# Sliding windows of an image batch: the second batch half shifted by one stride in SBUF, and half of each tile stored by SyncE

## The chip, the cores and the metric

The kernel runs on one core of a Trainium2 chip. The metric is the device time of one execution in microseconds. Before the change it is 185.93 us, the median of 3 runs (185.61 to 186.04). Engines are called as in the profile: DVE (VectorE), ACT (ScalarE), POOL (GpSimd), SP (SyncE, which only issues transfers here). The core has 16 DMA engines that all queues share.

## The reference

The input is 16 images of 64 channels and 64 x 64 pixels in float32. The output holds all windows of 8 x 8 pixels at a stride of 4, 15 x 15 of them, each with all channels:

```python
for i in range(n_h):          # n_h = n_w = 15
    for j in range(n_w):
        h_start = i * stride
        w_start = j * stride
        result[:, i, j] = x[:, :, h_start:h_start + 8, w_start:w_start + 8].copy()
```

Nothing is computed. 16.8 MB are read and 16 x 225 x 64 x 64 x 4 bytes = 59.0 MB are written. One output row, that is one window of one image with all channels, is 16 KB and contiguous in memory.

## The kernel before, in words

**Layout.** The input is loaded once into a tile `Lt`. A partition (lane) holds one image's band of 16 pixel rows for half of the channels: lane = channel half x 64 + image x 4 + band, with 4 bands per image. Images 0 to 7 (y = 0) and 8 to 15 (y = 1) therefore lie in groups of 32 lanes: channel half 0 has y = 0 in lanes 0 to 31 and y = 1 in 32 to 63, channel half 1 has them in 64 to 95 and 96 to 127. Each channel takes 1024 + 32 floats of a lane (L50 to L52).

**Loads.** The first 8 channels of each half are staged: ACT's and SP's queues load them into the four tile buffers `GG` (L115 to L118), and DVE and ACT copy them from there into `Lt` (L131 to L135). All other channels go straight to `Lt` (L120 to L126), in transfers of 8 lanes, by POOL's queue and six of them by SP's.

**Tiles.** The output is made in tiles of 128 lanes x 16 KB, each lane being one output row. There are four buffers in rotation (`tile_`, L193). DVE and ACT copy the windows of a tile out of `Lt` (both channel halves into one lane), and then one store sends the tile out. The vertical window positions of a band are slots s = 0 to 3 of the horizontal position j; s = 3 reaches four pixel rows into the next band, so its lower half comes from the next lane, by a `stream_shuffle` that moves lanes by one (`nxt`, L138). Tiles with such rows are called crossing here, the others inside the bands.

**Stores.** A tile leaves by an indirect transfer on POOL's queue (`scatter`, L146): each lane's target row is an index in a small tile (`idx` and others, computed on DVE in L75 to L104) plus a constant for s and j. An index out of range is dropped by the bounds check. That is used for the last band's crossing rows, which do not exist.

**Order.** The tiles are written out by hand. First three tiles of y = 0 alone (`part`, L198, two slots and two positions j at once), while the second half still loads. Then three times one full tile (`unit`, s = 0 in one half of the lanes and s = 1 in the other) and one `part` of y = 1. Then the loop (L237): three crossing tiles (s = 2 in one half of the lanes, s = 3 in the other, turning from tile to tile) and one inside the bands, five times. In the loop DVE copies by `stream_shuffle` with a mask that keeps each lane where it is (`shf`, L176). Last come two tiles of 64 lanes for j = 14, which SP stores with a plain transfer (L246 to L256):

```python
def unit(j, s, copies=(shf, mix)):
    g = tile_()
    if s == 0:
        fill(g, 0, 0, j, 0, HP, (act, copies[0]))
        fill(g, 1, 1, j, 0, HP, (act, copies[1]))
        scatter(g, idx, j, s)
    else:
        turn = 1 - crossed % 2
        fill(g, turn, s, j, 0, HP, (act, act))
        fill(g, 1 - turn, s + 1, j, 0, HP, (shf, mix))
        scatter(g, (idx_hi, idx_lo)[turn], j, s)
```

A fill of a buffer waits until the store four tiles earlier has landed. A store waits for all of its tile's copies. Stores do not wait for each other.

Of the kernel before, what the change touches and what calls it, by code (L numbers as in the profile page):

```python
# [10 lines left out]
def kernel(  # L11
# [7 lines left out]
    nc = tc.nc  # L19
# [30 lines left out]
    PAD = W // 2  # L50
    Lt = lpool.tile([P, CL, RB * W + PAD], f32)
# [16 lines left out]
    pi, tb, tq, tc_, th, idx, idx_y0, idx_y1, idx_lo, idx_hi = (  # L68
        itile(n) for n in ("pi", "tb", "tq", "tc", "th", "idx", "idx_y0", "idx_y1", "idx_lo", "idx_hi")
    )  # L70
    FAR = float(2 * B * NWIN)
    nc.gpsimd.iota(pi[:, :], pattern=[[0, 1]], base=0, channel_multiplier=1)  # L72
# [4 lines left out]
    def mul(d, a, m):  # L77
        nc.vector.tensor_scalar(out=d[:, :], in0=a[:, :], scalar1=float(m), scalar2=None, op0=ALU.mult)  # L78

    def tt(d, a, b, op):  # L80
        nc.vector.tensor_tensor(out=d[:, :], in0=a[:, :], in1=b[:, :], op=op)  # L81

    bits(tb, 2, B - 1)
    bits(tq, 0, HQ - 1)
    bits(tc_, 6, 1)
    mul(tb, tb, NWIN)
    mul(th, tq, NSLOT * NW)
    tt(tb, tb, th, ALU.add)
    mul(th, tc_, NW)
    tt(idx, tb, th, ALU.add)  # L90

    bits(th, 5, 1)
    mul(idx_y0, th, 1 - YB * NWIN)
    tt(idx_y0, idx_y0, idx, ALU.add)
    nc.vector.tensor_scalar(out=idx_y1[:, :], in0=idx_y0[:, :], scalar1=float(YB * NWIN), scalar2=None, op0=ALU.add)

    nc.vector.tensor_scalar(out=tq[:, :], in0=tq[:, :], scalar1=float(HQ - 1), scalar2=FAR, op0=ALU.is_equal, op1=ALU.mult)
    tt(th, tc_, tq, ALU.mult)
    tt(idx_hi, idx, th, ALU.add)
    nc.vector.tensor_scalar(out=tc_[:, :], in0=tc_[:, :], scalar1=-1.0, scalar2=1.0, op0=ALU.mult, op1=ALU.add)  # L100
    tt(th, tc_, tq, ALU.mult)
    tt(idx_lo, tb, th, ALU.add)
    mul(th, tc_, NW)
    tt(idx_lo, idx_lo, th, ALU.add)  # L104
# [7 lines left out]
    FC = NG * TC // CH  # L112
# [7 lines left out]
    for y in range(NY):  # L120
        for q in range(HQ):
            hw = y * HQ + q < HWP
            if hw:
                load(nc.sync, 0, y, q, FC + SMALL, CL)
# [54 lines left out]
    def split(k, other):  # L179
# [3 lines left out]

        return both

    mix = split(CL // 4, shf)


    EARLY = 3
# [102 lines left out]
```

## Time and profile before

| | |
|---|---|
| median of 3 runs | 185.93 us |
| the profiled execution | 186.0 us |
| its span in the profile | 184.2 us |
| DVE, ACT, POOL busy | 154.0 us (84%), 150.6 us (82%), 50.3 us (27%) |
| bytes moved by DMA | 75.81 MB |
| last DVE copy ends | about 175 us |

The profile shows one execution. Busy time of an engine is time in its instructions. The DMA row gives the busy share of the 16 DMA engines in each of 40 slices of the span, and queues are listed with the time that their packets took: `software_dynamic` is POOL's queue, the `hardware_dynamic` ones are SP's (q1) and ACT's (q10). A group of instructions is one line of the code, one engine and one shape, with the count, the busy sum, the mean of one in ns, and the idle time ahead of it with what ended that. A DMA issue's time to landing reaches from the issuing instruction until the last byte has been acknowledged. Beside the page, the trace holds a record of every DMA packet: its start, length, size and queue.

### The profile page before, as it was taken

How to read it: one execution, taken by the hardware profiler on the slowest of the kernel's cores; microseconds unless marked ns; L12 is line 12 of the kernel's file. 1: busy time of each engine (PE TensorE's matmuls, PEld its weight loads, DVE VectorE, ACT ScalarE, POOL GpSimd, SP SyncE). 2: the span in 40 equal slices, each digit the busy share in tenths (PEclk: the TensorE clock that was granted, in tenths of full speed). 3: DMA queues.
4: the chain of work that ended last, by engine and by line, in shares of the span. 5: the costliest groups of instructions: out<-in, count | busy, mean ns of one | idle time of the engine just before them, and what ended most of it. 6: DMA issues, size and time to landing. Idle time of an engine off the chain costs nothing.

```text
span 184.2 us, 597 instructions
## 1 busy us (share of the span) xinstructions
DVE 154.0 (84%) x213; ACT 150.6 (82%) x100; POOL 50.3 (27%) x50
## 2 busy tenths in 40 slices
DVE  5002998999989897999999999999999999999800
ACT  0002999999999999999899999998999999999600
POOL 7400763033353526111121112111211121114000
DMA  5999999999999999999999999999999999999995
GB/s 141 396 413 408 412 412 412 395 396 441 425 430 430 430 434 427 434 432 430 434 422 438 423 434 438 423 441 413 443 416 427 434 423 413 427 420 406 420 430 235
DMA packets 10980, 75.81 MB, mean 411 GB/s; under 512 B 3280, under 2 KB 3280, under 8 KB 7376
## 3 DMA queue, kind: packets, MB, share of 16 engines
q0 software_dynamic: 8656, 65.55, 84.8%
q1 hardware_dynamic: 1744, 8.13, 10.9%
q10 hardware_dynamic: 576, 2.10, 3.2%
q14 instruction: 4, 0.03, 0.0%
HBM read 16.78 MB, written 62.91 MB: 433 GB/s over the span
## 4 chain that ended last, share of the span: by engine, by line
DVE 53%; DMA 28%; issue 10%; POOL 2%; DVEq 1%; PEldq 0%
DVE GG L177 24%; DVE GG L170 16%; DMA out_dram<-GG,idx_y 14%; DMA Lt<-in_x_dram 14%; DVE GG L206 10%; DVE GG L254 3%; POOL Lt L61 2%; DVE GG L182 0%; DVEq L287 0%; DVE GG L167 0%; POOL pi L72 0%; DVEq L206 0%; PEldq L287 0%
## 5 line engine op out<-in xcount | busy, mean ns | idle before, releaser
L167 ACT COPY GG<-Lt 64x2048 f32<-64x2048 f32 x46 | 87.2, 1897 | 4.2 <-DMA out_dram<-GG,idx 1.8
L177 DVE STREAM_SHUFFLE GG<-Lt 64x1024 f32<-64x1024 f32 (+4 forms) x39 | 52.8, 1355 | 1.3
L206 DVE COPY GG<-Lt 32x2048 f32<-32x2048 f32 x30 | 36.6, 1219 | 3.4 <-DMA out_dram<-GG,idx_y 2.2
L170 DVE STREAM_SHUFFLE GG<-Lt 64x1024 f32<-64x1024 f32 x30 | 38.5, 1285 | 0.0
L206 ACT COPY GG<-Lt 32x2048 f32<-32x2048 f32 x18 | 34.1, 1897 | 0.8 <-DMA out_dram<-GG,idx_y 0.4
L135 DVE COPY Lt<-GG 32x2048 f32<-32x2048 f32 x10 | 11.9, 1234 | 13.8 <-DMA GG<-in_x_dram 13.7
L61 POOL DMA_DIRECT2D Lt<-in_x_dram x16 | 13.7, 868 | 17.8 <-DMA Lt<-in_x_dram 17.3
L147 POOL DMA_INDIRECT out_dram<-GG,idx_y x6 | 10.1, 1690 | 26.3 <-DVE GG L206 17.6
L147 POOL DMA_INDIRECT out_dram<-GG,idx x8 | 11.7, 1463 | 17.5 <-DVE GG L177 13.3
L147 POOL DMA_INDIRECT out_dram<-GG,idx_lo x8 | 7.7, 964 | 30.2 <-DVE GG L170 15.1
L135 ACT ACT_TABLE_LOAD x1 | 1.3, 1283 | 17.3 <-DMA GG<-in_x_dram 17.3
L147 POOL DMA_INDIRECT out_dram<-GG,idx_hi x7 | 6.7, 963 | 26.5 <-ACT GG L167 11.4
L135 ACT COPY Lt<-GG 32x2048 f32<-32x2048 f32 x6 | 11.2, 1894 | 0.1
L181 ACT COPY GG<-Lt 64x256 f32<-64x256 f32 (+2 forms) x21 | 10.2, 484 | 0.5
L167 DVE COPY GG<-Lt 64x2048 f32<-64x2048 f32 x6 | 7.3, 1222 | 0.2
L254 ACT COPY GG<-Lt 32x768 f32<-32x768 f32 x8 | 6.6, 828 | 0.1
L254 DVE COPY GG<-Lt 32x1280 f32<-32x1280 f32 x8 | 6.6, 819 | 0.1
L75 DVE TENSOR_SCALAR tb<-pi 128x1 int32<-128x1 int32 x1 | 0.2, 154 | 1.0 <-POOL pi L72 1.0
L182 DVE COPY GG<-Lt 64x1280 f32<-64x1280 f32 x1 | 0.9, 875 | 0.0
L81 DVE TENSOR_TENSOR th<-tc,tq 128x1 int32<-128x1 int32 x2 | 0.3, 156 | 0.0
L78 DVE TENSOR_SCALAR th<-tc 128x1 int32<-128x1 int32 x2 | 0.3, 154 | 0.0
L72 POOL IOTA pi<- 128x1 int32 x1 | 0.1, 125 | 0.4 <-PEq L287 0.4
(21 smaller groups left out, 3.1 us busy)
## 6 DMA issues: line engine op xcount, KB each, us to landing
Lt<-in_x_dram POOLq DMA_DIRECT2D x10, 768.0 KB, 17.9
Lt<-in_x_dram SPq DMA_DIRECT2D x6, 640.0 KB
GG<-in_x_dram SPq DMA_DIRECT2D x4, 512.0 KB, 14.8
GG<-in_x_dram ACTq DMA_DIRECT2D x4, 512.0 KB, 14.5
out_dram<-GG SPq DMA_DIRECT2D x2, 1024.0 KB, 9.5
Lt<-in_x_dram POOLq DMA_DIRECT2D x6, 128.0 KB, 17.8
out_dram<-GG,idx POOLq DMA_INDIRECT x8, 11.9
out_dram<-GG,idx_lo POOLq DMA_INDIRECT x8, 9.5
```

The costliest lines, as they stand in the source:

```text
L61: eng.dma_start(out=L[p0 : p0 + QP - HQ + 1 : HQ, c0:c1, :, :], in_=x_v[ch, y, q, :, c0:c1, :])
L78: nc.vector.tensor_scalar(out=d[:, :], in0=a[:, :], scalar1=float(m), scalar2=None, op0=ALU.mult)
L81: nc.vector.tensor_tensor(out=d[:, :], in0=a[:, :], in1=b[:, :], op=op)
L135: tc.keep_in_program_order(copy(out=L[d, c : c + PC, :, :], in_=S[ch][f, c : c + PC]))
L147: st = nc.gpsimd.indirect_dma_start(out=o_v, out_offset=bass.IndirectOffsetOnAxis(ap=ix[:, 0:1], axis=0), in_=g.rearrange("p c r w -> p (c ...
L167: copy(out=g[d, cs, :, :], in_=L[f, :, s * ST : s * ST + WS, cols])
L170: nc.vector.stream_shuffle(out=g[d, cs, ST:WS, :], in_=L[f, :, 0:ST, cols], mask=nxt)
L177: nc.vector.stream_shuffle(out=out, in_=in_, mask=same)
L181: act(out=out[:, 0:k], in_=in_[:, 0:k])
L182: other(out=out[:, k:], in_=in_[:, k:])
L206: (act if n % 3 == 0 else dve)(out=g[d * QP : (d + 1) * QP, ch * CL : (ch + 1) * CL, :, :], in_=L[f : f + QP, :, s * ST : s * ST + WS, cols],)
L254: copy(out=g[d, ch * CL + c0 : ch * CL + c1, :, :], in_=L[f, c0:c1, s * ST : s * ST + WS, cols])
```

## The change

The second batch half (y = 1) is stored four elements, which is one stride, further on in each channel of `Lt`, and the two batch halves change places in the lanes. `L` becomes two views of the same tile, `L[0]` from element 0 and `L[1]` from element 4. A copy that runs over 64 lanes of `L[0]` at position j reads window j of y = 0 and window j - 1 of y = 1; over `L[1]` it reads window j of y = 1 and window j + 1 of y = 0.

So a full tile is one slot s for all lanes: the first 64 lanes come from `L[0]`, the others from `L[1]`, and the middle 64 lanes (32 to 95) hold window j of all 16 images, in the order of one plain transfer. In tiles inside the bands (s = 0, 1, 2) SP stores the middle 64 lanes, and a scatter with the index `sw` stores the outer 64, whose middle indices are out of range. Crossing tiles (s = 3) go out by one scatter with the index `sx`. Positions j go in steps of two; the tiles at the edges (j = 0 or 6, and j = 14) fill 96 lanes and have indices of their own.

The copies of a tile inside the bands are one of 2048 elements by ACT, two by DVE's plain copy, and one shared half and half. In a crossing tile ACT copies the upper four rows of all four parts, and DVE shuffles the lower four. The copies by a shuffle that keeps the lanes, and the two half tiles at the end, are gone. One channel fewer of the upper channel half is staged (7 instead of 8), and POOL's loads of that half grow by one channel. The index arithmetic on DVE has 29 instructions instead of 20. The early tiles (`part`) stay.

```diff
-    L = Lt[:, :, 0 : RB * W].rearrange("p c (r w) -> p c r w", r=RB)
+    L = [Lt[:, :, n * ST : n * ST + RB * W].rearrange("p c (r w) -> p c r w", r=RB) for n in range(2)]
...
+    def lanes(ch, y):
+        p0 = ch * HP + (NY - 1 - y) * QP
+        return slice(p0, p0 + QP)
...
     def load(eng, ch, y, q, c0, c1):
-        p0 = ch * HP + y * QP + q
-        eng.dma_start(out=L[p0 : p0 + QP - HQ + 1 : HQ, c0:c1, :, :], in_=x_v[ch, y, q, :, c0:c1, :])
+        p0 = lanes(ch, y).start + q
+        eng.dma_start(out=L[y][p0 : p0 + QP - HQ + 1 : HQ, c0:c1, :, :], in_=x_v[ch, y, q, :, c0:c1, :])
...
-    FC = NG * TC // CH
+    FC = (NG * TC // CH, NG * TC // CH - 1)
...
-            load(nc.gpsimd, 1, y, q, FC, CL)
+            load(nc.gpsimd, 1, y, q, FC[1], CL)
...
-    ACT_C = 12
+    ACT_C = CL // 2
...
-    def unit(j, s, copies=(shf, mix)):
-        nonlocal crossed
+    o_e = out.rearrange("b i j c r w -> j b i (c r w)")
+
+    def unit(j, s):
         g = tile_()
-        if s == 0:
-            fill(g, 0, 0, j, 0, HP, (act, copies[0]))
-            fill(g, 1, 1, j, 0, HP, (act, copies[1]))
-            scatter(g, idx, j, s)
-        else:
-            turn = 1 - crossed % 2
-            crossed += 1
-            fill(g, turn, s, j, 0, HP, (act, act))
-            fill(g, 1 - turn, s + 1, j, 0, HP, (shf, mix))
-            scatter(g, (idx_hi, idx_lo)[turn], j, s)
+        lo = j > (2 * EARLY if s < 2 else 0)
+        hi = j < NW - 1
+        cross = s == NSLOT - 1
+        cols = slice(j * ST, j * ST + WS)
+        for h in range(CH):
+            a, b = (0 if lo else QP, HP) if h == 0 else (0, HP if hi else QP)
+            d = slice(h * HP + a, h * HP + b)
+            for n, ch in enumerate((h, 1 - h)):
+                f = slice(ch * HP + a, ch * HP + b)
+                cs = slice(ch * CL, (ch + 1) * CL)
+                if cross:
+                    act(out=g[d, cs, 0:ST, :], in_=L[h][f, :, s * ST : RB, cols])
+                    nc.vector.stream_shuffle(out=g[d, cs, ST:WS, :], in_=L[h][f, :, 0:ST, cols], mask=nxt)
+                else:
+                    copy = (act, dve, dve, split(ACT_C))[h * CH + n]
+                    copy(out=g[d, cs, :, :], in_=L[h][f, :, s * ST : s * ST + WS, cols])
+        g_q = g.rearrange("p c r w -> p (c r w)")
+        if not cross:
+            free(nc.sync.dma_start(out=o_e[j, :, s : s + (HQ - 1) * NSLOT + 1 : NSLOT], in_=g_q[QP : QP + HP]))
+        outer = ((sw, sx), (sw_lo, sx_lo), (sw_hi, sx_hi))[0 if lo and hi else 1 if lo else 2]
+        scatter(g, outer[cross], j, s)
...
-    while plain:
-        for w in cross[:3]:
-            unit(*w)
-        cross = cross[3:]
-        unit(*plain.pop(0), *([] if len(plain) else [(split(ACT_C, shf), split(ACT_C, dve))]))
+    while cross:
+        unit(*cross.pop(0))
+        unit(*below.pop(0))
+        if len(plain) > len(cross):
+            unit(*plain.pop(0))
-    j = NW - 1
-    for s in range(2):
...
-        free(nc.sync.dma_start(out=o_e[j, :, s : s + (HQ - 1) * NSLOT + 1 : NSLOT], in_=g_q[QP : QP + HP]))
```

More of the change, by code (lines that the diff above doesn't have):

```diff
@@ L230 @@
     for n in range(EARLY):
         part(0, 2 * n)
[L232 to L233 removed]
+    last = NW - 1
+    js = [2, last, 0, *range(4, last, 2)]
+    below = [(j, NSLOT - 2) for j in js]
+    cross = [(j, NSLOT - 1) for j in js]
+    js = list(range(2 * EARLY + 2, last, 2))
+    plain = [(j, s) for j in js[:-1] for s in range(2)]
+    plain += [(j, s) for s in range(2) for j in (last, 2 * EARLY, js[-1])]
     for n in range(EARLY):
[L235 removed]
+        unit(*plain.pop(0))
```

117 lines of the change are left out of this document (47 added, 70 removed).

## The prediction, made before the change was run

> **What bounds the kernel now.** I read the page's DMA part first, because 75.8 MB pass in 184.2 us.
>
> ```profile
> DMA  5999999999999999999999999999999999999995
> ...
> DMA packets 10980, 75.81 MB, mean 411 GB/s; under 512 B 3280, under 2 KB 3280, under 8 KB 7376
> ...
> q0 software_dynamic: 8656, 65.55, 84.8%
> q1 hardware_dynamic: 1744, 8.13, 10.9%
> q10 hardware_dynamic: 576, 2.10, 3.2%
> ```
>
> The three queues together hold 98.9% of the span of all 16 DMA engines. Then the busy time by stage, for which I chose stretches by what the kernel does (loads to 45 us, early tiles to 76, the loop to 170, drain):
>
> ```profile
> core 0: us, DVE busy (x) ACT busy (x) POOL busy (x), PEclk, DMA share, GB/s
> ...
> 45.00:76.00 31.00, 28.22 (x24) 30.27 (x17) 12.37 (x6) 1.00 1.01 431
> 76.00:150.00 74.00, 72.87 (x113) 70.27 (x51) 15.43 (x16) 1.00 1.01 430
> 150.00:160.00 10.00, 9.87 (x17) 9.87 (x7) 1.93 (x2) 1.00 1.00 421
> 160.00:170.00 10.00, 9.84 (x15) 9.30 (x10) 2.97 (x3) 1.00 0.98 411
> ```
>
> Here DVE is 98% busy and DMA is full too. Which one paces? The groups price a tile, and the DMA issues and waits show who is ahead:
>
> ```profile
> L167 ACT COPY GG<-Lt 64x2048 f32<-64x2048 f32 x46 | 87.2, 1897 | 4.2 <-DMA out_dram<-GG,idx 1.8 <-DMA out_dram<-GG,idx_hi 0.6 <-DMA out_dram<-GG,idx_y 0.6
> L170 DVE STREAM_SHUFFLE GG<-Lt 64x1024 f32<-64x1024 f32 x30 | 38.5, 1285 | 0.0
> L167 DVE COPY GG<-Lt 64x2048 f32<-64x2048 f32 x6 | 7.3, 1222 | 0.2
> L177 DVE STREAM_SHUFFLE GG<-Lt 64x2048 f32<-64x2048 f32 x4 | 9.7, 2420 | 0.1
> ```
> ```profile
> out_dram<-GG,idx_lo POOLq DMA_INDIRECT x8, 9.5
> ```
>
> A store lands 9.5 us after its issue, while a tile of 128 rows is 2.10 MB, so 4.87 us at 431 GB/s: about two tiles stand in the queue. The chain of waits runs 53% through DVE, yet the DMA queue hides it. Only towards the end of the loop does the queue run thin (0.98, 411 GB/s). So the kernel is **bound by the DMA engines**, and DVE becomes the bound at 160 us.
>
> The packet records of the trace say the same in smaller units. On one DMA engine, 16 KB rows start 607 ns apart (16 x 16,384 B / 607 ns = 432 GB/s), 4 KB load packets 155 ns, and a 4-byte packet delays the next by 6 ns. There are 3280 of the last kind. They close each DMA (one on each engine it uses), stand in on idle engines for loads of 8 partitions, and stand for each scatter row that the bounds check drops: a crossing tile shows 6 rows and 2 such packets on half of the engines.
>
> **The change, part by part.** The sum is made against the profiled execution: 186.0 us, of which 184.2 span and 1.8 around it; that is 0.07 over the median 185.93.
>
> *Rows and tiles.* Stored bytes stay: 3600 rows. Tiles were 29 scatters and 2 half tiles by SP; they become 6 early tiles, 18 inside bands (the middle 64 lanes by SP, the rest by scatter) and 8 crossing ones, so 32 scatters and 18 SP stores. SP carries 18 x 64 = 1152 rows (was 128), scatters 2448.
>
> *Dropped rows.* Of 32 x 128 = 4096 scatter slots 1648 are dropped, against 15 x 16 = 240 before. 1408 more at 6 ns over 16 engines: **+0.53 us**. Nothing hides this on a full engine.
>
> *Closing packets.* 32 + 18 DMAs for 29 + 2: 19 more, one packet on each engine: **+0.11 us**.
>
> *Rows that go by SP.* In the records SP's 16 KB packets took 617 ns on average, scatters' 614 (median 611). Bounds for 1024 moved rows: 0 (the same row gap) and, if all rows inside bands (some 140 per engine) get 6 ns longer by alternating between two queues as in the drain, 0.84. I take **+0.3**, nearest to the 3 ns between the means.
>
> *DVE and ACT.* The loop from 76 us stores 2448 rows in either kernel: 2448 x 607 ns / 16 = 92.9 us of DMA. DVE had 15 crossing tiles x (1.281 + 0.998 + 2 x 1.285) + plain tiles 19.5 + SP's half tiles 6.6 = 98.8 us, 6 us more than DMA; the queue built up before covered it until 160 us. After: a tile inside a band costs DVE 2 x 1.222 and 64x1024 (some 0.7 between the 1280 and the 2048 rows), 3.15; a crossing one 4 x 1.285 = 5.14. The sum is 15 x 3.15 + 8 x 5.14 = 88.4; ACT (1.897 + 1.04, and 4 x 1.04) 77.4. Both fall below DMA, so the thin end goes. What it cost: against 430 GB/s the stretches of 150 to 178 us lost (9 x 10 + 19 x 10 + 6 x 8) / 430 = 0.76 us; by the records the engines stood idle 0.37 us on average. Between these ends I take **-0.5**. Late next is the DMA queue, which is why ten us of DVE work buy no more. The early alternation costs DVE 6.2 + 3.15 = 9.4 us for 9.7 us of DMA: still covered.
>
> *Index arithmetic.* Nine more DVE instructions of some 0.15 us before 6 us: hidden, since DVE then waits 13.7 us for staged data.
>
> *One staged channel less.* SP's four staged loads lose a 4 KB packet per lane (4 packets fewer on each engine), and POOL's 8 loads of the upper channels grow from 24 to 25. Those loads run on 8 of the 16 engines (the records: 8 chains of pure loads beside 8 that mix SP's loads). So that half does 4 packets more net, +0.62 us, and the other 0.62 less. Before, the other half trailed by 0.65 us after the loads and then stored two rows fewer per engine (8 crossing tiles dropped on its side, 7 on the other), ending 0.56 ahead. After, stores are even and it is 0.54 ahead. The skew is equal: **0**, +-0.3.
>
> *Four elements further on.* Half of the loads now land 16 B off. Nothing in the trace has such a transfer. Nearest row: the channel pitch of 4224 B already puts odd channels 128 B off, and load packets are 158 to 159 ns for nearly all. So 0; the upper end is a load packet doubled, 98 x 155 ns = 15 us. I take **0**, by the nearest row. The Trainium skill (DMA: Bandwidth & Descriptors, How a descriptor splits into AXI transactions) charges the bytes from the 256 B boundary below the start: half a 32 B beat, so one beat more on 128. By that rule, an estimate, the sum would be 0.12 us higher; no run here shows it.
>
> *Waits.* SP's store waits for the whole fill and only later stores stand behind it. POOL's scatter waits for the same fill. Buffers wait for both stores; as the queues alternate by row, a crossing tile behind half a tile is released up to 4 rows, 2.4 us, later. Of about 17 us between two uses of a buffer, fill (4.2), issue (2), the tile's own rows (4.3) and landing leave more than that: 0, at worst some +1 around the short edge tiles.
>
> Sum: 0.53 + 0.11 + 0.3 - 0.5 = +0.44: 186.0 + 0.4 = **186.4 us**, 0.2% over the profiled execution and 0.25% over the median.
>
> **Rivals.**
>
> *Uneven lanes (slower).* I assume that the 64 outer lanes spread over all engines, 4 rows each. Were engines given 8 neighbouring lanes, scatters inside bands would fall on 8 engines: 285 rows there against 225 on average, 60 x 0.607 = +36 us, 222 us. Every engine dropping 2 of 8 in a crossing half fits both maps. For mine speaks that each engine's rows keep 607 ns in full tiles. 6%. [...]
>
> *Late scatters (slower).* Scatter issue took 1690 ns on POOL beside DVE's copies and 963 beside shuffles, and the change puts copies where shuffles were. If the queue held less than one tile, 26 scatters would expose up to 0.73 us each, +19 us; with the queue two tiles deep nothing. It decides once landing times fall under some 7 us. I price a part of it, the edge tiles, or a few ns on each unaligned load: 187.5 to 190 us, 14%. The Trainium skill (SBUF — State Buffer, the box on SWDGE under "SBUF: two separate sides") says that such copies lock POOL out while it writes descriptors; the two durations agree. By it alone, with every scatter exposed, 205 us.
>
> *Two queues help (faster).* When loads and stores mixed (41 to 45 us) the records show packets overlapping, and one stretch of 4 us moved 441 GB/s. If rows of two queues overlap likewise, 87 us of tiles inside bands (144 rows per engine) shorten by up to 2%, -1.8: 184.6 us. With half of it, and the full 0.76 of the thin end, 185.2. Against it: SP's and scatter's rows alternating in the drain took 611 to 625 ns. 22%.
>
> *Nothing to see.* The terms are small; with 0 for alternation and -0.76 for the thin end the sum is -0.1: 185.9.
>
> **How the numbers follow.** Bounds of the likeliest case (58%, which holds "nothing to see"): 0.64 + 0 - 0.76 - 0.3 = -0.4 to 0.64 + 0.84 - 0.37 + 0.3 = +1.4, so 185.6 to 187.4. Taking in most of the faster rival and the near half of late scatters: 185.0 to 188.2, which leaves out 6% uneven lanes, about 8% late scatters or loads, 5% below. A measurement of this kernel tells 0.2% (0.37 us) from no change. Slower by more: 32 of the 58, and 6 + 14: 52%. Within: 25%. Faster: 22 of the rival and 1 more: 23%.
>
> **What would show it.** Right: DMA share 1.00 at about 430 GB/s through 170 us, DVE waiting for stores in the loop, 1400 more small packets, landing near 10 us. Wrong: a stretch of the loop under 415 GB/s (uneven lanes or late scatters), load stretches under 398 GB/s (the 16 B), or over 435 with both store queues busy (two queues help).

## The result, and the profile after

The changed kernel takes 192.04 us (median of 4 runs, 192.00 to 192.08) against 185.99 us, a ratio of 1.0329 with a 95% interval of 1.0312 to 1.0347. It is slower, as the likelier side of the prediction had it, but by 6 us instead of 0.4, and outside the predicted range. The span of the profiled execution grows from 184.2 to 190.2 us.

The first view is the DMA part of the page of the changed kernel, the counterpart of what opened the prediction. Its row has one digit for each 4.8 us.

```profile
DMA  5999999999999999999999899799999999999991
...
DMA packets 12756, 75.81 MB, mean 399 GB/s; under 512 B 5056, under 2 KB 5056, under 8 KB 9152
...
q0 software_dynamic: 9216, 49.04, 62.8%
q1 hardware_dynamic: 2960, 24.64, 31.1%
q10 hardware_dynamic: 576, 2.10, 3.0%
```

The bytes are the same. The queues hold 96.9% of the DMA engines' span instead of 98.9%, there are 1776 more small packets, and two digits in the middle (8 and 7, at 105 and 119 us) say that the DMA engines ran dry twice. Before, that row had no digit below 9 between the ends. The second view, busy time by stretches, puts numbers on it:

```profile
core 0: us, DVE busy (x) ACT busy (x) POOL busy (x), PEclk, DMA share, GB/s
45.00:76.00 31.00, 27.55 (x25) 24.79 (x15) 9.99 (x6) 1.00 1.01 431
76.00:100.00 24.00, 23.25 (x30) 20.63 (x18) 7.72 (x6) 1.00 1.00 425
100.00:125.00 25.00, 22.63 (x29) 21.43 (x18) 8.39 (x7) 1.00 0.93 388
125.00:150.00 25.00, 23.03 (x29) 18.77 (x16) 8.54 (x7) 1.00 1.00 415
150.00:160.00 10.00, 7.34 (x10) 6.00 (x5) 3.09 (x3) 1.00 1.01 416
160.00:170.00 10.00, 9.65 (x13) 9.56 (x8) 1.74 (x3) 1.00 1.00 416
```

From 45 to 76 us nothing has changed (431 GB/s in either kernel), although rows of SP and of the scatters alternate there already. After that two different things are to be seen. From 100 to 125 us the share falls to 0.93: nothing to send. From 125 us on the share is 1.00 again but only 415 GB/s pass, where it was 430: the rows take longer.

In the groups, DVE and ACT have become as light as the prediction worked out (DVE 154.0 to 148.1 us, ACT 150.6 to 132.1), and yet they wait:

```profile
L225 DVE COPY GG<-Lt 64x2048 f32<-64x2048 f32 (+1 forms) x36 | 44.3, 1231 | 7.5 <-issue 4.8
L225 ACT COPY GG<-Lt 64x2048 f32<-64x2048 f32 (+1 forms) x18 | 34.2, 1899 | 18.5 <-issue 11.7
L222 DVE STREAM_SHUFFLE GG<-Lt 64x1024 f32<-64x1024 f32 (+1 forms) x32 | 40.8, 1274 | 1.2
```

Some of these waits are for a buffer that comes free late. The view names `issue`, but DVE's wait of 1.73 us that ends at 109.27 us, for one, ends 0.08 us after the landing (109.19 us) of the store that had used the buffer before.

**Where the 6.0 us of span are.** The trace's packet records allow a full account, in us per DMA engine (a sum over all packets divided by 16). A record does not name its engine; with 16 engines, "dry" counts how many packets fewer than 16 are under way at a time, and "overlap" how many more:

| | before | after | difference |
|---|---|---|---|
| dry: fewer than 16 packets under way, from the first to the last | 1.08 | 3.23 | +2.15 |
| 3600 rows of 16 KB, mean length 614.1 and 619.2 ns | 138.17 | 139.33 | +1.16 |
| small packets, 3280 and 5056 of 9.0 ns | 1.85 | 2.85 | +1.00 |
| load packets, 164.4 and 164.7 ns | 42.08 | 42.17 | +0.09 |
| overlap: more than 16 under way, taken off | 2.39 | 2.66 | -0.27 |
| end: last landing to end of span | 0.93 | 2.80 | +1.87 |

So three accounts have to be explained: dry spells, long rows, and the end. A fourth is hidden by the mean over all load packets. Those that start between 32 and 36 us, which all load the shifted half y = 1, take 160 ns on average in the five runs with the old layout and 166 in the 14 with the new one; before 28 us they take 160 in all of them. The stretch, before and after:

```profile
32.00:36.00 4.00, 3.88 (x4) 3.95 (x3) 0.46 (x1) 1.00 1.04 410
```
```profile
32.00:36.00 4.00, 3.91 (x4) 3.95 (x3) 0.92 (x1) 1.00 1.04 393
```

For the 98 shifted packets of an engine 4 to 6 ns more are some 0.5 us, an estimate. The table shows only 0.09, mostly because ACT's staged packets came out shorter in this execution (175.0 ns instead of 181.5; 173 to 181 in runs of either layout).

**The end.** POOL closes with a drain that ends 1.9 to 2.0 us after its last scatter has landed, and where nothing else is late the span ends 0.8 us after the drain. Before the change, the last scatter landed at 181.02 us, the drain ended at 182.91, and SP's last store landed at 183.30: the drain was covered. After it, SP's last store landed at 184.97, the last scatter at 187.44, the drain ended at 189.45 and the span at 190.24: nothing covers it.

### The profile page after: what moved, and what is told of

The parts are those of the page before. It is cut to its first block, busy times and chain, and to the rows that moved or that the text cites. A ratio compares the mean times of both kernels' runs of the same rounds, so it can differ in the third digit from the quotient of the medians.

```text
span 190.2 us, 629 instructions
## 1 busy us (share of the span) xinstructions
DVE 148.1 (78%) x187; ACT 132.1 (69%) x93; POOL 61.2 (32%) x53
## 2 busy tenths in 40 slices
DMA packets 12756, 75.81 MB, mean 399 GB/s; under 512 B 5056, under 2 KB 5056, under 8 KB 9152
## 3 DMA queue, kind: packets, MB, share of 16 engines
HBM read 16.78 MB, written 85.98 MB: 540 GB/s over the span
## 4 chain that ended last, share of the span: by engine, by line
DMA 76%; DVE 11%; issue 5%; SPq 1%; POOLq 1%; DVEq 0%
DMA out_dram<-GG,sw 46%; DMA Lt<-in_x_dram 12%; DVE GG L225 7%; DMA out_dram<-GG,idx_y 6%; DMA GG<-in_x_dram 6%; DMA out_dram<-GG,sw_lo 4%; DMA out_dram<-GG,sw_hi 3%; DVE GG L176 2%; SPq L133 1%; DVE GG L222 1%; POOLq L279 1%; SPq L66 0%; DVE GG L196 0%; DVEq L279 0%; DVEq L222 0%
## 5 line engine op out<-in xcount | busy, mean ns | idle before, releaser
L225 DVE COPY GG<-Lt 64x2048 f32<-64x2048 f32 (+1 forms) x36 | 44.3, 1231 | 7.5 <-issue 4.8
L225 ACT COPY GG<-Lt 64x2048 f32<-64x2048 f32 (+1 forms) x18 | 34.2, 1899 | 18.5 <-issue 11.7
L222 DVE STREAM_SHUFFLE GG<-Lt 64x1024 f32<-64x1024 f32 (+1 forms) x32 | 40.8, 1274 | 1.2
L221 ACT COPY GG<-Lt 64x1024 f32<-64x1024 f32 (+1 forms) x32 | 33.4, 1043 | 0.9 <-ACT GG L175 0.2
L160 POOL DMA_INDIRECT out_dram<-GG,sw x12 | 15.8, 1320 | 21.9 <-DVE GG L176 10.8
L150 DVE COPY Lt<-GG 32x2048 f32<-32x2048 f32 (+1 forms) x10 | 11.4, 1181 | 13.0 <-DMA GG<-in_x_dram 12.9
L175 ACT COPY GG<-Lt 64x1024 f32<-64x1024 f32 (+1 forms) x18 | 18.8, 1043 | 0.4
L160 POOL DMA_INDIRECT out_dram<-GG,sx x6 | 10.7, 1782 | 25.7 <-ACT GG L225 12.8
L176 DVE COPY GG<-Lt 64x1024 f32<-64x1024 f32 (+1 forms) x18 | 12.4, 687 | 0.6
L150 ACT COPY Lt<-GG 32x2048 f32<-32x2048 f32 (+1 forms) x6 | 10.3, 1752 | 0.1
L160 POOL DMA_INDIRECT out_dram<-GG,sw_lo x3 | 3.8, 1283 | 6.7 <-DVE GG L176 6.7
## 6 DMA issues: line engine op xcount, KB each, us to landing
GG<-in_x_dram SPq DMA_DIRECT2D x4, 448.0 KB, 13.4
```

The lines of the kernel that those rows point to most:

```text
L150: tc.keep_in_program_order(copy(out=L[y][lanes(ch, y), c:e, :, :], in_=S[ch][f, c:e]))
L160: st = nc.gpsimd.indirect_dma_start(out=o_v, out_offset=bass.IndirectOffsetOnAxis(ap=ix[:, 0:1], axis=0), in_=g.rearrange("p c r w -> p (c ...
L175: act(out=out[:, 0:k], in_=in_[:, 0:k])
L176: dve(out=out[:, k:], in_=in_[:, k:])
L221: act(out=g[d, cs, 0:ST, :], in_=L[h][f, :, s * ST : RB, cols])
L222: nc.vector.stream_shuffle(out=g[d, cs, ST:WS, :], in_=L[h][f, :, 0:ST, cols], mask=nxt)
```

## The experiments

Each ratio is to the kernel before on the same chip, with the 95% interval in brackets. "Dry" is the first row of the table above. The edits are to the changed kernel unless another is named; `...` marks lines left out. The theory to start with was: **the edge tiles throw the DMA engines apart.** Tiles of j = 14 leave out one outer side of 32 lanes, those of j = 0 and 6 the other, so eight engines run some rows ahead of the eight others; the slowest engine decides when a buffer comes free. In the changed kernel the first engine had finished the short store issued at 96.6 us at 101.78 us and the last one at 109.19 us; for the full store issued at 99.9 us this spread was 4.9 us. Before the change it was 0.8 to 2.7 us throughout. The rival: DVE and ACT can't supply enough tiles, wherever the edge tiles are.

**1. Exchange two edge tiles** (a1), so that lower tiles of opposite sides stand beside the crossing ones.

```diff
-    below = [(j, NSLOT - 2) for j in js]
+    below = [(j, NSLOT - 2) for j in (2, 0, last, *range(4, last, 2))]
```

> Only the order of two edge tiles inside the bands changes (j = 0 comes where j = 14 stood, and the other way round), so the sizes of the tiles and the work of DVE and ACT follow in the same order. Skew theory: edge tiles give 3 or 4 rows more to one half of the DMA engines; in the changed kernel two of them in a row lean to the same side by 7 rows (4.2 us), a buffer is then held by the late half while the other half runs dry. With the swap the lean stays at 4 rows or less, so the first dry spell (106 to 110 us, 0.7 us of idle on average) should nearly go and the second (118 to 122 us, 1.3 us) shrink: 190.0 to 191.0 us. Supply theory (the edge tiles cost DVE and ACT as much as full ones but carry fewer rows): nothing that it counts has changed, 191.9 to 192.2 us.

190.70 us, 1.0275 [1.0258, 1.0292]: in the range of the theory of drift. The first dry spell is gone, the second one (118 to 122 us) stays; dry 1.94.

**2. Pair the plain edge tiles too** (a2): the above, and `plain` in the order of 14 and 6 side by side.

```diff
-    plain += [(j, s) for s in range(2) for j in (last, 2 * EARLY, js[-1])]
+    plain += [(js[-1], 0), (last, 0), (2 * EARLY, 0), (last, 1), (2 * EARLY, 1), (js[-1], 1)]
...
-        if len(plain) > len(cross):
+        for _ in range({6: 1, 5: 1, 3: 2, 1: 2, 0: 1}.get(len(cross), 0)):
```

> The order of the loop's tiles alone changes: edge tiles that lean to opposite halves of the DMA engines follow each other directly, and full tiles are spread so that each group has about as much DMA as DVE time. Both the skew and the supply theory expect the dry spells to go: idle of the DMA engines 3.2 us (with start and end) falls to about 1.2, and if longer rows come from restarts after dry spells, the mean row record falls from 619 to about 612 ns, another -1.4 us. Together 188.4 to 189.0 us; 190.0 if rows stay long. Rival (queues of SP and POOL that alternate hold buffers too long whatever the order): 191.5 to 192.2 us.

190.46 us, 1.0261 [1.0244, 1.0279]: missed, no better than the exchange alone. Dry is 2.80, now between 142 and 157 us, in the profiled execution, which at 191.4 us is the longest of the five (the others took 190.3 to 190.5). Its trace shows what is behind it: a crossing tile's scatter issued at 125.13 us landed at 138.11, while SP's half of the next tile, issued at 127.65, had landed at 136.30. The later store of the other queue overtakes, and the crossing tile's buffer is held; DVE then waited 4.2 us for it. Drift alone is not the whole, in this execution at least.

**3. Leave out the last scatter** (e1); its 64 rows are not stored.

```diff
-            unit(*plain.pop(0))
+            unit(*plain.pop(0), len(plain) > 0)
```

> The changed kernel without the scatter of its very last tile: 64 of the 3600 rows are left out, SP's store of the same tile stays and is the last transfer. Theory: when a scatter is the last transfer to land, POOL's closing drain ends 1.9 to 2.0 us after that landing and SP works through nine waits in a row, so the span ends 2.75 us after the last landing against 0.87 before; with SP's store last this goes: -1.9 us, and the missing rows -2.4 us (64 x 607 ns / 16): 187.7 us. Rival: the end costs the same whoever is last: -2.4 us alone, 189.6 us.

188.90 us, 1.0178 [1.0161, 1.0195]: by the ratios 2.8 us less than the changed kernel, not 4.3. The scatter before it landed at 184.38 us, only 0.6 us ahead of SP's store, and the drain ended 1.97 us later, so it was hardly covered: the end fell from 2.80 to 2.14 us. The drain's 2.0 us hold; the test of the end was not clean.

**4. Only the DVE relief, in the kernel before** (b1): the shuffles that keep each lane become plain copies.

```diff
-        nc.vector.stream_shuffle(out=out, in_=in_, mask=same)
+        nc.vector.tensor_copy(out=out, in_=in_)
```

> The kernel before, with plain copies on DVE in place of the shuffles that keep the lanes; nothing else. DVE then needs about 20 us less in the loop. Theory (DMA bound, and rows become longer only after a dry spell): the DMA engines never run dry before the end (0.37 us back) and rows stay at 611 to 612 ns (0.6 us back): 184.9 to 185.3 us. Rival (plain copies hold up POOL's descriptors, scatter issue 0.96 to 1.7 us, and that shows): 186.0 to 187.5 us. If rows grow longer at about 126 us all the same, their growth isn't from dry spells: 185.6 us.

186.34 us, 1.0037 [1.0023, 1.0052]: not faster, a little slower. The stretches of this kernel (columns as above, here and below):

```profile
45.00:76.00 31.00, 28.37 (x24) 30.61 (x17) 11.86 (x6) 1.00 1.01 432
76.00:150.00 74.00, 55.73 (x87) 70.84 (x51) 19.62 (x17) 1.00 1.01 429
150.00:160.00 10.00, 7.59 (x13) 8.67 (x7) 1.92 (x2) 1.00 1.01 424
160.00:170.00 10.00, 5.50 (x7) 9.22 (x10) 2.61 (x2) 1.00 1.00 426
```

DVE falls from 72.87 to 55.73 us in the loop, and the last stretch does rise from 411 to 426 GB/s. The thin end is gone: between 160 and 168 us the DMA engines had been dry for 0.23 us, and now they are not. But dry is 1.55 against 1.08, because the engines finish less evenly (1.22 us in the last 3 us, where it was 0.43), and the rows are as long as before (614.2 ns). So the relief brought its 0.23 us and the end took more; why the engines finish less evenly stays open.

**5. One queue** (c1): each tile leaves whole by one scatter, with an index `sf` for all 128 lanes. And **6.** the same with the exchange of a1 (c2).

```diff
...
-        if not cross:
-            free(nc.sync.dma_start(out=o_e[j, :, s : s + (HQ - 1) * NSLOT + 1 : NSLOT], in_=g_q[QP : QP + HP]))
-        outer = ((sw, sx), (sw_lo, sx_lo), (sw_hi, sx_hi))[0 if lo and hi else 1 if lo else 2]
+        outer = ((sf, sx), (sf_lo, sx_lo), (sf_hi, sx_hi))[0 if lo and hi else 1 if lo else 2]
```

> The changed kernel with its layout, tiles, order and copies, but every tile leaves whole by one scatter, as in the kernel before; SP stores nothing. Queue theory (two store queues alternate by row, so SP's halves of later tiles overtake the scatter of a crossing tile and its buffer is held until they have passed): stores land in order of issue again, DVE and ACT wait less for buffers. Idle of the DMA engines 3.2 us falls to between 1.0 (nothing but the start) and 2.0 (what the lean of the edge tiles leaves), and 1152 dropped rows fewer save 0.43 us; the closing drain of POOL stays: 189.3 to 190.6 us. Supply theory (edge tiles short of rows whatever the queue): idle stays near 3 us, only the dropped rows go: 191.5 us. If rows still grow longer after 95 us their growth is not from alternating queues.

> As the one-queue kernel, with the two edge tiles of j = 0 and j = 14 inside the bands exchanged, so that leans to one half of the DMA engines cancel. Queue and skew theory together: no dry spell is left (idle about 1.0 us, the start), and what remains over the kernel before is POOL's drain (1.9 us) and longer rows: 188.2 to 189.2 us. If dry spells stay although the order of landing and the lean are mended, both theories are short of something: over 190 us.

190.57 us, 1.0265 [1.0248, 1.0282], and 189.59 us, 1.0207 [1.0189, 1.0224]. The second is slightly above its range. One queue is better than two by 0.6%, and the exchange brings another 0.6%. The packets of c1:

```profile
DMA packets 11316, 75.81 MB, mean 401 GB/s; under 512 B 3616, under 2 KB 3616, under 8 KB 7712
...
q0 software_dynamic: 9216, 67.91, 86.5%
```

It has 1440 small packets fewer than the changed kernel and no alternation of queues in the loop, and still its rows grow to a mean of 618.3 ns, against 619.2. Neither the 1152 dropped rows that are gone here nor alternation is what makes most of the changed kernel's rows long.

**7. Dropped rows alone** (d1): b1 with 11 scatters added among the early tiles whose 128 indices are all out of range.

```diff
+    def dropped(n=1):
+        for _ in range(n):
+            scatter(G[(at - 1) % NG], idx_far, 0, 0)
...
```

> The kernel before with plain copies (measured at 1.0037 of the kernel before), and on top of it 11 scatters of which all 128 rows are dropped, issued among the early tiles: 1408 dropped rows more, exactly as many as the change adds, and nothing else. Packet theory (6 ns each on one of 16 engines, and 11 closing packets): +0.6 us, ratio 1.007. Rival: a dropped row costs far more than its packet, for instance it reads its 16 KB, as the byte counter of the page counts them as written: several us, up to +53 us. Rival: they hide altogether: 1.0037.

189.44 us, 1.0199 [1.0182, 1.0216]: 3.0 us over b1, five times the price of the prediction. Its stretch with the added scatters:

```profile
45.00:76.00 31.00, 27.40 (x23) 29.74 (x17) 27.04 (x14) 1.00 0.99 408
```

432 GB/s in b1 are 408 here. By the records the packets themselves cost 0.88 us and longer rows 2.43. Half of that (1.2 us) lies between 56 and 92 us, while dropped rows are sent: rows take 633 ns on average there instead of 611. The other half lies behind the last of them, where rows do not come back to 611 ns. In the changed kernel dropped rows come 64 at a time, and c1, with 1152 fewer, saves only 0.2 us of row length: there they cost little more than their own time.

**8. and 9. The end with SP last** (f1, f2), on top of a1: SP's half of the last lower tile is held back.

```diff
-            free(nc.sync.dma_start(out=o_e[j, :, s : s + (HQ - 1) * NSLOT + 1 : NSLOT], in_=g_q[QP : QP + HP]))
+            o_m = o_e[j, :, s : s + (HQ - 1) * NSLOT + 1 : NSLOT]
+            if hold is None:
+                st = nc.sync.dma_start(out=o_m, in_=g_q[QP : QP + HP])
+                tc.keep_in_program_order(st)
+                free(st)
+            else:
+                hold += [o_m, g_q[QP : QP + HP]]
...
+    st = nc.sync.dma_start(out=held[0], in_=held[1])
```

> The changed kernel with the two edge tiles exchanged (measured at 1.0275 of the kernel before) and one more move: SP's store of the last but two half tiles, 64 rows of the last tile below the crossing ones, is issued after SP's store of the very last tile, so that the scatters land some 2.4 us before SP's last rows. All rows are stored. End theory (POOL's closing drain ends 2.0 us after the last scatter's landing, in six of six traces, and only counts when a scatter lands last): -1.5 to -1.9 us, ratio 1.0175 to 1.0195, and the span ends about 0.9 to 1.3 us after the last landing. Rival (the wait at the end follows whatever lands last): 1.0275.

> The changed kernel with the two edge tiles exchanged (1.0275 of the kernel before), and now with SP's order of stores fixed so that the store of the last tile below the crossing ones really goes out after SP's store of the very last tile (in the earlier try the SP stores came in their old order: the scatter still landed last, by 2.5 us, so that run tells nothing of the end). All rows are stored. End theory (POOL's closing drain ends 2.0 us after the last scatter's landing, and counts only when a scatter lands last): -1.2 to -1.9 us, ratio 1.0172 to 1.021. Rival (the end waits as long whatever lands last): 1.0265 to 1.0275.

190.56 us, 1.0265 [1.0248, 1.0282], and 191.06 us, 1.0291 [1.0274, 1.0308]: both missed. In f1 (which moved the store in the text but did not fix SP's order) the stores were issued as in a1, so it is a repetition of a1. In f2 (the diff above) SP's store landed at 186.23 us, but the last scatter at 186.43: they share the DMA engines, so the scatter moved back as the store did, and the drain ended 2.0 us after it again.

**10. No dropped rows** (g2): b1 without the tiles that drop rows; 784 of the 3600 rows are not stored.

```diff
-            fill(g, turn, s, j, 0, HP, (act, act))
-            fill(g, 1 - turn, s + 1, j, 0, HP, (shf, mix))
-            scatter(g, (idx_hi, idx_lo)[turn], j, s)
+            fill(g, 0, s, j, 0, HP, (act, shf))
+            fill(g, 1, s, j + 1, 0, HP, (act, mix))
+            scatter(g, idx_j, j, s)
```

> The kernel before with plain copies, and with no dropped rows at all: all rows of slot s = 3 and those of s = 2 at j = 14 are left out (784 of 3600), and tiles of s = 2 carry two neighbouring positions instead. Question: what makes a 16 KB row take 618 to 630 ns instead of 611 from some point on (126 us in the kernel before, 93 us in the changed one, 57 us with dropped rows added early)? Dropped-row theory: rows stay at 611 ns to the end at about 151 us (786 fewer rows x 607 ns / 16 = 29.8 us less than 184). Time or place theory (the amount written, the position j): they grow at about 126 us here too, to 615 or more by 135 us.

157.06 us, which is no ratio to compare, since less is stored. The rows stay at 611 ns until 128 us and then take 612 to 618; in the kernel before and in b1 they leave 611 ns at 124 to 128 us as well. Dropped rows therefore don't set that moment in the kernel before. Nor does drift here: with every tile full, the spread between the first and the last engine's landing is 1.74 to 1.82 us in all 19 stores issued up to 124 us, the last of which landed at 138.3, and 3.1 us in the next one. The rows grow first.

**11. Two scatters of 32 lanes for the outer lanes** (h1, on a1), so that nothing is dropped inside the bands.

```diff
-        scatter(g, outer[cross], j, s)
+        if cross:
+            scatter(g, outer, j, s)
+        if not cross and lo:
+            scatter(g, sw, j, s, slice(0, QP))
+        if not cross and hi:
+            scatter(g, so, j, s, slice(P - QP, P))
...
```

> The changed kernel with the two edge tiles exchanged (1.0275 of the kernel before); the outer lanes of a tile inside the bands go out by two scatters of 32 lanes each instead of one of 128 lanes of which 64 are dropped. So 1152 dropped rows go, and 14 scatters come. Dropped-row theory: packets -0.43 us, and rows stay at 611 ns longer, up to -1.2 us more: 189.0 to 190.2 us, mean row record under 615 ns. Rival (rows grow longer for another reason): 190.3 us, rows as before at 618 to 619. If a scatter of 32 lanes uses few of the DMA engines, the lean between engines grows and the time goes over 192 us.

Between 253.6 and 261.0 us in four executions, 1.3742 [1.3646, 1.3839] from the two shorter ones; the trace is of the longest. The rows of such a scatter do spread over all 16 engines, two each, so that is not the cause. The spread of landings grows with each of them, to 8.97 us for the scatter issued at 59.9 and 12.8 us for that issued at 61.2, rows take 700 to 1050 ns on average in many stretches of 4 us, and the engines are dry for 42 us. Why, stays open.

**12. Drift alone, in the kernel before** (k3): the side on which crossing tiles drop 16 rows doesn't turn from tile to tile.

```diff
-            turn = 1 - crossed % 2
+            turn = int(not 4 <= crossed < 11)
```

> The kernel before, with only the sides of its crossing tiles set in another order: the side on which 16 rows are dropped no longer turns from tile to tile, but stays for four tiles, then for seven on the other side, then for four. Rows, packets, dropped rows and copies are the same. Each crossing tile gives eight DMA engines 2 rows less than the others, 1.2 us, so the engines drift apart by up to 4.9 us. Theory of drift: rows of 16 KB grow from 611 to over 616 ns soon after 95 us (before: at 126 us) and dry spells of the DMA engines grow, together 1 to 2.5 us, ratio 1.005 to 1.014. Rival, drift is harmless and rows grow for another reason: the rows grow at about 126 us as before and the ratio is 0.998 to 1.002.

186.69 us, 1.0053 [1.0039, 1.0067]: drift alone costs time, at the lower end of what the theory gave. The spread of landings reached 5.6 us, and where it did the engines ran dry. The stretches of this kernel, and then of the kernel before:

```profile
140.00:150.00 10.00, 9.89 (x15) 8.92 (x7) 1.92 (x2) 1.00 0.94 395
```
```profile
140.00:150.00 10.00, 9.85 (x15) 9.01 (x8) 1.93 (x2) 1.00 1.01 429
```

Dry is 1.66 against 1.08. The rows leave 611 ns at 112 to 116 us instead of 128, but grow little (615.1 ns on average, against 614.1).

**13. and 14. The crossing and lower edge tiles late** (c3 with one queue, a3 with two).

```diff
-    js = [2, last, 0, *range(4, last, 2)]
+    js = [*range(2, last - 2, 2), last, 0, last - 2]
```

> The changed kernel with every tile stored whole by one scatter, and the crossing and the lower tiles of j = 14 and j = 0 moved from the beginning of the loop towards its end, ahead of those of j = 12. Theory of drift: rows stay at 611 to 613 ns until about 140 us (with one queue and the edge tiles early they grew from 100 us on), the dry spells at 106 to 122 us go, and 1.6 to 2.8 us are saved against the one-queue kernel: ratio 1.011 to 1.018. Rival, rows grow for another reason and dry spells come wherever the edge tiles are: 1.022 to 1.028.

> The changed kernel with two queues as it is, and only the crossing and the lower tiles of j = 14 and j = 0 moved towards the end of the loop, ahead of those of j = 12. Theory of drift: the dry spells at 106 to 122 us go and rows grow later, 1.5 to 2.8 us less than the changed kernel, ratio 1.018 to 1.025. Rival, two queues drift apart by themselves: rows grow at 95 us as in the changed kernel, ratio 1.028 to 1.034.

192.16 us, 1.0343 [1.0329, 1.0357], and 194.30 us, 1.0460 [1.0446, 1.0474]: slower than with the edge tiles early, against both theories' ranges. The stretches of c3:

```profile
100.00:125.00 25.00, 21.23 (x25) 18.53 (x15) 9.16 (x6) 1.00 1.01 427
125.00:150.00 25.00, 22.32 (x28) 20.11 (x16) 7.92 (x6) 1.00 1.01 425
150.00:160.00 10.00, 9.11 (x13) 7.59 (x7) 2.82 (x2) 1.00 0.81 336
170.00:178.00 8.00, 5.93 (x6) 4.53 (x4) 4.68 (x3) 1.00 0.81 338
```

The dry spells have left 100 to 125 us and followed the edge tiles. Six of the eight short tiles now stand in a row (stores issued at 144.8 to 163.5 us), and dry is 4.68. The rows of c3 speak against drift as what makes them grow: they leave 611 ns at 108 us (622 ns at 110 to 114), while the spread stays at 1.5 to 1.6 us until a store whose first engine landed at 121.69.

Hence a second cause beside drift: **a short tile takes a buffer and the filling time of a full one, but only 96 / 128 of its transfer** (3.7 instead of 4.9 us). Several in a row empty the queue. A crossing tile is short in the same sense wherever it is: a quarter of its rows does not exist, so it sends 96, or 72 at the edges, for 5.2 us of shuffles. In the changed kernel three short tiles stand between the stores issued at 105 and 113 us, with 72, 96 and 96 rows, 10.1 us of transfer at 611 ns a row. The crossing tile behind them was issued only at 118.5 us, 13.4 us after the first of the three, and its first landing came at 124.95. That is the second dry spell:

```profile
116.00:120.00 4.00, 3.90 (x5) 3.93 (x4) 1.53 (x1) 1.00 0.88 365
120.00:124.00 4.00, 3.88 (x5) 3.93 (x4) 2.19 (x2) 1.00 0.79 332
```

These are stretches of the changed kernel. DVE and ACT are 97 to 98% busy in them: they work at full speed for a queue that ran empty over the tiles before.

A third part is in the issue of that crossing tile. Its shuffles ended at 117.70 us, the scatter ran from 118.47 to 120.33, beside DVE's plain copies for the next tile, and its rows began at 120.90, when all engines had been idle since 120.5. Before the change, scatters of crossing tiles ran beside shuffles and took half as long (a line of the page of before, then two of after):

```profile
L147 POOL DMA_INDIRECT out_dram<-GG,idx_lo x8 | 7.7, 964 | 30.2 <-DVE GG L170 15.1
```
```profile
L160 POOL DMA_INDIRECT out_dram<-GG,sx x6 | 10.7, 1782 | 25.7 <-ACT GG L225 12.8
...
118.47 1.86 POOL L160 DMA_INDIRECT out_dram<-GG,sx  x1 [4.28 <-ACT GG L225]
```

The engines' idle time in the 0.9 us before the first rows is 0.84 us here and 0.4 us behind the crossing store of 105.09 us, also 1.86 us long. So the longer issue may be worth 1.3 of the 2.0 us of both dry spells, an estimate; no run changes it alone.

**15. Short tiles taken apart** (n2): one queue, and the loop's 23 tiles in a list in which no two short ones are neighbours and the sides take turns.

```diff
+    loop = [(2, 3), (2, 2), (14, 0), (4, 3), (4, 2), (6, 0), (6, 3), (10, 1), (14, 2), (8, 3), (6, 2), (0, 2)]
+    loop += [(8, 2), (14, 3), (12, 0), (10, 2), (0, 3), (12, 1), (14, 1), (10, 3), (6, 1), (12, 3), (12, 2)]
...
+    for w in loop:
+        unit(*w)
```

> The changed kernel with every tile stored whole by one scatter (as in the one-queue run, 1.0265) and the loop's 23 tiles in another order: of the eight short tiles of 96 lanes (j = 0, 6 and 14) never two in a row, and the two sides in turn. Theory of short tiles and drift: dry spells of the DMA engines fall from 2.6 to below 1.4 us, rows grow no sooner than at 110 us; 1.5 to 2.2 us less than the one-queue kernel, ratio 1.014 to 1.019. Rival, dry spells come from the crossing tiles' long fills whatever the order: 1.022 to 1.028.

189.36 us, 1.0198 [1.0184, 1.0212]: 1.2 us less than c1, where 1.5 to 2.2 were expected; the rival's range is excluded. Dry falls from 2.60 to 1.76 us, mean row length from 618.3 to 616.3 ns, and the middle of the loop is whole. The order parts the short tiles and turns the sides at once, so it does not tell the two causes apart. Of what is left, 0.9 us lies behind the crossing stores issued at 164.0 and 172.5 us.

```profile
100.00:125.00 25.00, 22.71 (x29) 20.59 (x17) 9.36 (x7) 1.00 1.01 429
125.00:150.00 25.00, 20.89 (x28) 18.71 (x16) 7.87 (x6) 1.00 1.00 419
```

**16. and 17. The last tile whole by SP** (n1 on the changed kernel, n3 on n2): its outer lanes leave by two plain transfers of 32 lanes; all rows are stored.

```diff
+        if end:
+            for h, y in ((0, 1), (1, 0)):
+                o_y = o_e[j - 1 + 2 * h, y * B // NY : (y + 1) * B // NY, s : s + (HQ - 1) * NSLOT + 1 : NSLOT]
+                free(nc.sync.dma_start(out=o_y, in_=g_q[h * (P - QP) : h * (P - QP) + QP]))
+            return
...
```

> The changed kernel, with its very last tile stored whole by SP: its outer lanes leave by two plain transfers of 32 lanes in place of the scatter. All rows are stored. The last scatter is then that of the tile before it. Theory of the end: POOL's closing drain ends 2.0 us after the last scatter's landing, which now lies some 2 to 4 us ahead of SP's last landing, so the end of the span comes 0.8 to 0.9 us after the last landing instead of 2.75: 1.5 to 1.9 us less than the changed kernel, ratio 1.022 to 1.025. Rival, the end costs the same whichever queue lands last, because another instruction waits as long: 1.031 to 1.034.

> The spread order with one scatter for each tile, and the last tile stored whole by SP in three plain transfers. If both theories hold, the two gains add: 3 to 4 us less than the one-queue kernel, ratio 1.004 to 1.011. If the end costs nothing that SP can cover, as the spread order alone.

192.28 us, 1.0357 [1.0343, 1.0371], and 190.54 us, 1.0262 [1.0248, 1.0276]: both missed, although the end did what the theory says. In n1 the last scatter landed at 185.20 us, the drain ended at 187.17, covered by SP's last landing at 189.21, and the span ended 1.29 us after that instead of 2.80. The gain was given back by the transfers themselves. The end of n1:

```profile
178.00:184.00 6.00, 0.00 (x0) 0.00 (x0) 0.00 (x0) 1.00 1.00 421
184.00:186.00 2.00, 0.00 (x0) 0.00 (x0) 0.00 (x0) 1.00 0.54 188
186.00:190.50 4.50, 0.00 (x0) 0.00 (x0) 0.00 (x0) 1.00 0.27 117
```

A share near one half: the records show both stores of 32 lanes on the same eight engines, 4 rows each. From 184.5 us on only eight packets are under way; the other eight engines had nothing left. Dry grew from 3.23 to 4.88 us, 1.65 against the 1.5 that the end gained.

No version came out ahead of the kernel before. The nearest, n2, has a span of 187.4 us, 3.2 over it: by the same accounts the end is 1.9 of that, dry spells 0.7, longer rows 0.5 and small packets 0.2.

## Why the prediction was wrong, step by step

**Waits: the step that failed.** "0, at worst some +1 around the short edge tiles" came out at +2.15 us. The prediction saw the place, and compared the wrong quantities: it asked whether a buffer's mean time between two uses suffices, and whether DVE's sum over the loop (88.4 us) stays below DMA's (92.9), not what a run of short tiles leaves in the queue, nor that a buffer is freed by its slowest engine. By its own prices a crossing tile costs DVE 5.14 us for 96 rows, 3.64 us of DMA. Four mechanisms were found. Drift: a1 takes the first spell away, and k3 makes one in the kernel before. Short tiles in a row: c3 moves the dry spells with them, and n2 takes most of them out, together with drift. Two queues, of which the later store can overtake the earlier: c1 without them is 1.2 us faster than the changed kernel by the ratios, of which its fewer small packets are at most 0.8. And the longer issue of crossing scatters, which is an estimate from the trace. How the 2.15 us divide among them is not shown.

**The end: a step that was missing.** The prediction summed the DMA work and put the end at nothing without a reason. It cost 1.9 us, because the scatter has become what lands last; e1, n1 and n3 each show the drain of 2.0 us behind the last scatter, and n1 that a later landing of SP's covers it (in n3 it covers all but 0.15 us).

**Rows that go by SP: wrong in kind.** Alternation costs nothing while it is alone: from 54 to 80 us rows of both queues take 611 ns. The rows do grow, by 1.16 us in all, above the upper bound of 0.84, but c1 has most of that growth (0.94) with one queue. They also grow in the kernel before, from 128 us on, and in b1 without dry spells in the loop. In k3, where drift alone was added, they leave 611 ns some 12 to 16 us earlier, which fits drift as one cause. It is not the cause in general: in c3 and g2 the rows grow before the landings spread. What makes a row longer stays open.

**Dropped rows and closing packets: about right here.** 0.64 us were expected of them together; the records give 1.00 of length, 0.73 if all of the added overlap is put to them. That a dropped row costs only its own packet isn't general: d1 shows 3.0 us for the same number in bursts of 128.

**DVE and ACT: the gain of 0.5 didn't come.** The busy times were worked out well, but b1, which has that relief alone, is 0.4% slower than before. The low figures at 150 to 170 us were real, but only 0.23 us of them was idle DMA, which b1 wins back. The rest is mostly the rows' growth, which stayed in b1, and b1's end takes more than was won.

**Four elements further on: 0 was too little.** The late load packets take some 4 to 6 ns more in every run with the new layout, some 0.5 us in all by estimate, and the stretch from 32 to 36 us falls from 410 to 393 GB/s. That is one of the signs that the prediction named, though the whole load phase to 45 us passes 398 GB/s in both kernels. The two batch halves also changed lanes, and no run separates this from the 16 B. The Trainium skill (DMA: Bandwidth & Descriptors, How a descriptor splits into AXI transactions), by which the prediction had estimated 0.12 us, speaks of bytes that are fetched; here the shifted side is the one that is written, and what was measured is several times more.

**Right**: bytes, the numbers of stores and the index arithmetic; nothing speaks against the staged channel.

**The rivals.** *Uneven lanes* didn't happen: in a scatter inside the bands each engine carries four outer and four inner rows. But n1's plain stores of 32 lanes do what that rival feared. *Late scatters* happened in part. POOL's issues of crossing tiles became longer beside copies (1782 ns on average with `sx`, 964 before), and where the queue ran thin that came out in full: stores land a median of 11.1 us after issue by the view, but those issued between 112.5 and 121.0 us land after 6.7 to 7.6, about the 7 us that the prediction named. *Two queues help* is refuted by c1. The sign on which the prediction said that it would be wrong, a stretch of the loop below 415 GB/s, did show (388). Of the two causes that it named for it, late scatters hold in part; short tiles and drift were not named. That the kernel came out slower, as the sum said, is luck in good part: 4.0 of the 6.0 us, the dry spells and the end, were put at nothing in it.

## What to carry to other kernels

When DMA is the bound, the work to sum is that of each DMA engine and each tile in its order: a tile that fills a buffer at the full price and moves less empties the queue, and several in a row do so however good the mean is. Ask of the last few microseconds which queue lands last and what that queue's engine still has to do, since nothing behind it covers it. A change that relieves an engine standing behind a full queue brings little, even where that engine is 98% busy. And what a deep queue hides, such as a longer issue, counts again where the queue runs thin.

## What the runs showed of the hardware that was not expected

- POOL's closing drain ends 1.9 to 2.0 us after its last scatter has landed in nearly all traces (1.6 in g2, 2.3 in d1, 2.5 in h1).
- A plain store of 32 lanes of 16 KB (8 images of 4 rows) went out on eight of the 16 DMA engines, a second one on the same eight (n1). The plain stores of 64 lanes (16 images of 4 rows) and the 32 or 64 valid rows of a scatter spread evenly over all 16 (two or four each).
- A dropped row goes out as a packet of 4 bytes. 1408 of them in whole scatters made the rows among them 22 ns longer on average (d1), and the rows behind them stayed longer too.
- A crossing tile's scatter took 0.96 us to issue beside shuffles and mostly 1.86 beside DVE's plain copies. With a full queue that did not show; behind short tiles the engines stood idle meanwhile (the store of 118.5 us).
- Load packets of the half that lies 16 B off and in other lanes took 166 ns from 32 to 36 us, where they took 160 before.
- The page's counter of bytes written to memory rose from 62.91 to 85.98 MB with unchanged stores: 1408 dropped rows x 16,384 B are 23.07 MB. It counts dropped rows as written.
- 30 scatters of 32 lanes in place of 18 with 64 (in six of them 32) valid rows took the kernel to 254 us and more (h1), for a reason that stays open.
